# Delta rule: q's rows and the output's columns turned by VectorE blocks and GpSimd transfers through DRAM

## The chip, the cores and the metric

The kernel runs on one core of one Trainium2 chip. The core has TensorE (PE, matrix products into PSUM), VectorE (DVE), ScalarE (ACT), GpSimd (POOL) and SyncE (SP), and 16 DMA engines that the queues of SP, ACT and POOL share. The metric is the device time of one execution in microseconds (us): 2160.38 us as the median of 3 runs (2159.5 to 2160.82) for the kernel before.

## The reference

One inference step of a decoder layer for 512 prompt tokens and 8 sample tokens, width 2048. A normed input is multiplied with one matrix whose columns are q, k, v, an output gate z, two small gate columns, and the pooling channels. Eight heads of width 128 run a gated delta rule, four pooling groups run beside them; both go through one output matrix, and a SwiGLU block and a final norm follow. What the change touches, for each head of the prompt:

```python
q = l2norm(q) * (DN_HEAD_DIM ** -0.5)        # one factor for each token
...
# chunk by chunk:
v_new = u_i - einsum('bhck,bhkv->bhcv', w_i, S)
o = einsum('bhck,bhkv->bhcv', q_i * exp(g_i), S) + einsum('bhcs,bhsv->bhcv', qk_i, v_new)
S = S * exp(g_last) + einsum('bhck,bhcv->bhkv', k_dec, v_new)
...
dn_out = rmsnorm(o, dn_norm) * silu(z)
```

Products come out of the input projection with channels on partitions and tokens along the free dimension. The norm of q needs, for each token, the sum over channels, as a column with the token on the partition. The output o comes out with tokens on partitions, and the output projection needs it with channels on partitions.

## The kernel before

All matrix products are made in two float32r parts of each operand ("hi" and "lo"), three passes for each product. In the first part of the program, one "tile" is 128 output columns of the input matrix for all 520 tokens: 16 steps over the contraction, each with two column halves and three passes (lines 168 to 170), and the second half three steps behind the first. The weights come in granules of 128x1024 by SP's queue, are cut into hi by ScalarE (line 135) and lo by VectorE (line 137), and the products are evicted by VectorE (line 259).

After nearly each step `weave.step()` is called (class `Weave`): it runs generators on tracks, each of which issues a few small instructions and yields the number of steps until it goes on. So the small work of the heads stands between the matmuls of the big products, in the order in which the generators are run. For TensorE this order is kept as it is written; on the other engines a scheduler sets the order from what is issued, with priorities.

Two batches of four heads: for each batch four k tiles, four z tiles, and then for each head a q tile and a v tile, after which `delta(h, qT, vT)` is put on track 0. It takes some 26 steps, and so runs during the q and v tiles of the next head. It

- multiplies q with the decay (line 825), multiplies the inverse's parts (lines 831, 850) with the copy `xt_` between them (line 833, ScalarE) and `uu` (line 852, VectorE),
- turns q with four TensorE transposes (line 838), so that ScalarE sums the squares of each token out of PSUM (line 757, called at 840) and a root by GpSimd (line 215, called at 843) gives the factor `fq`,
- runs four chunks of 128 tokens, each with the matmuls of lines 877, 884, 889, 895 and 896, and the state `S` written by VectorE (line 892 for chunk 0, line 894 for others); line 877 of the next chunk waits for `S`,
- sums the squares of the output (line 902), takes the root `ro`, scales the output into `on`, a part of `mixb` (line 910), and puts `gate(h, on)` on track 1.

`gate` turns `on` with four TensorE transposes (line 916) and multiplies the result with the norm's weights and the gate (line 918) into `mix[h]`. After the heads come eight pooling tiles, with the last head's recurrence, the sample tokens' products and the pooling products (`pool_mix`, track 1) woven into them, and the output projection. The feed-forward part follows, and takes most of the time.

Of the kernel before, what the change touches and what calls it, by code (L numbers as in the profile page):

```python
# [8 lines left out]
F32 = mybir.dt.float32  # L9
F32R = mybir.dt.float32r  # L10
I32 = mybir.dt.int32
AF = mybir.ActivationFunctionType
# [21 lines left out]
HG = 8  # L34
BUFS = {
    "ext": 2, "y": 1, "ys": 1, "g3": 3, "junk": 1, "ss": 2, "rr": 2, "nb": 1, "u": 1, "tm": 2, "xt_": 1, "uu": 2,
    "qts": 1, "fq": 2, "aq": 1, "vs": 1, "R": 2, "W": 2, "S": 2, "so": 2, "ro": 2, "s0": 2, "s2": 1, "kd": 4, "st": 2,
}
SKEW = 3
AHEAD = 2000  # L40
# [2 lines left out]
class Weave:  # L43
# [1 line left out]


    def __init__(self):
        self.tracks, self.wait, self.now = ([], []), [0, 0], 0

    def add(self, task, track=0, delay=0):  # L50
        self.tracks[track].append((task, self.now + delay))
# [18 lines left out]
def decoder_kernel(ctx, tc, x_prompt, x_sample, state_delta, state_conv, state_pool, norm_mix, w_in,  # L70
# [17 lines left out]
    def pst():  # L88
        return ps_dn.tile([P, 512], F32, tag="dn", name="dn")
# [431 lines left out]
    with ExitStack() as p1:  # L521
# [204 lines left out]
        def ck(c):  # L726
            return slice(P * c, P * (c + 1))


        def qkv_tile(sec, h, out, ext=None):  # L730
# [9 lines left out]
            act.activation(out, y, AF.Silu)  # L740
            pool.tensor_copy(ccp[:, :, t], ext[:, SEQ:SEQ + 3])

        def decay(h):

            gcb = d1tile("g3", [P, SEQ], "gcb")
            sp.dma_start(gcb, gcr_d[h:h + 1, :].broadcast_to([P, SEQ]))
            dm = d1tile("g3", [P, SEQ], "dm")
            for c in range(NCH):
                dve.scalar_tensor_tensor(dm[:, ck(c)], gcb[:, ck(c)], gcs[:, c, h:h + 1], mneg,
                                         op0=ALU.subtract, op1=ALU.min)  # L750
            act.activation(dm, dm, AF.Exp)
            return gcb, dm
# [64 lines left out]
        def delta(h, qT, vT):  # L817
# [15 lines left out]
            act.copy(xt_, v3(xp)[:, :, 0:96])  # L833
            cur = d1tile("uu", [P, SEQ], "uu")
            pool.tensor_copy(v3(cur), udf)
            qtp = pst()
            for c in range(NCH):
                te.transpose(qtp[:, ck(c)], qT[:, ck(c)], ident)
            ss = d1tile("ss", [P, NCH], "ss")
            squares(qtp, ss)  # L840
            dve.tensor_scalar(ss, ss, EPS, None, op0=ALU.add)
            fq = d1tile("fq", [P, NCH], "fq")
            pow_mhalf(fq, ss)
            dve.tensor_scalar(fq, fq, float(P) ** -0.5, None, op0=ALU.mult)
            yield 2
            for it in range(3):
                yp = v3(pst())
# [24 lines left out]
            for c in range(NCH):  # L872
                if S is None:
                    R = vs[:, ck(c)]
                else:
                    kp = pst()
                    te.matmul(kp[:, 0:P], kT[:, ck(c)], S, start=True, stop=True)
                    Rt = d1tile("R", [P, P], "R")
                    dve.scalar_tensor_tensor(Rt, kp[:, 0:P], negc[:, c, h:h + 1], vs[:, ck(c)],
                                             op0=ALU.mult, op1=ALU.add)  # L880
                    R = Rt
                    yield 2
                wp = pst()
                te.matmul(wp[:, 0:P], cur[:, ck(c)], R, start=True, stop=True)
                W = d1tile("W", [P, P], "W")
                act.copy(W, wp[:, 0:P])
                yield 2
                dp = pst()
                te.matmul(dp[:, 0:P], kd[:, ck(c)], W, start=True, stop=True)
                S2 = d1tile("S", [P, P], "S")  # L890
                if S is None:
                    dve.tensor_copy(S2, dp[:, 0:P])
                else:
                    dve.scalar_tensor_tensor(S2, S, egl[:, c, h:h + 1], dp[:, 0:P], op0=ALU.mult, op1=ALU.add)
                    te.matmul(op_[:, ck(c)], qts[:, ck(c)], S, start=True, stop=False)
                te.matmul(op_[:, ck(c)], aq[:, ck(c)], W, start=(S is None), stop=True)
                S = S2
                yield 1
            sp.dma_start(nd_prompt[0, 0, h], S)

            so = d1tile("so", [P, NCH], "so")
# [6 lines left out]
            dve.tensor_tensor(ro, ro, fq, op=ALU.mult)  # L908
            on = nn
            dve.tensor_tensor(v3(on), v3(op_), bc3(ro), op=ALU.mult)  # L910
            weave.add(gate(h, on), 1, 8)

        def gate(h, on):
            otp = pst()
            for c in range(NCH):
                te.transpose(otp[:, ck(c)], on[:, ck(c)], ident)
            yield 1
            dve.scalar_tensor_tensor(mix[h][:, NB:NTOK], otp, dnw, mix[h][:, NB:NTOK], op0=ALU.mult, op1=ALU.mult)

# [167 lines left out]
        def qv_tiles(h):  # L1089
            utf = utfs[h % 2].rearrange("p a c j -> p (a c) j")  # L1090
            for q in range(4):
                r = slice(32 * q, 32 * q + 32)
                sp.dma_start(utf[r, :, r], ud_d[h, q].rearrange("a c s j -> s (a c) j"))
            qT = d1tile("s0", [P, SEQ], "qT")
            qkv_tile(0, h, qT)
            vT = d1tile("s2", [P, SEQ], "vT")
            qkv_tile(2, h, vT)
            weave.add(delta(h, qT, vT), 0, 1)

        kds = {}  # L1100
        for b in range(2):
            for h in range(4 * b, 4 * b + 4):
                qkv_tile(1, h, mixb[:, h % 4, 0:SEQ],
# [27 lines left out]
        for t in (6, 7, 4, 5, 2, 3, 0, 1):  # L1131
            pool_tile(t, operands)
            if t % 2:
                weave.add(pool_mix(t // 2, *splits[t // 2]), 1, 12 if t > 1 else 7)
        weave.add(pool_out(), 0, 6)

        order = [*range(8), 14, 15, 12, 13, 10, 11, 8, 9]
# [939 lines left out]
```

## Time and profile before

| what | value |
|---|---|
| median of 3 runs | 2160.38 us (2159.5 to 2160.82) |
| profiled execution, first to last instruction | 2158.9 us |
| TensorE busy | 2136.1 us (99%) |
| VectorE busy | 1746.4 us (81%) |
| ScalarE busy | 929.6 us (43%) |
| GpSimd busy | 433.8 us (20%) |
| the four recurrences of a batch (about) | 160 to 290 us, and 388 to 518 us |

Times in a timeline are us from the span's start; a row is start, duration, engine, line and instruction, and in brackets the idle time of the engine before it and what ended it. A matmul's duration runs from its start to the end of its flow through the array, so matmuls that follow each other overlap; the distance from one start to the next is what one takes from the engine. A group's row has busy time and mean ns of one, then the idle time before.

### The profile page before, as it was taken

The page shows a single profiled execution, that of the slowest core. Times are in us where ns is not written, and L with a number is a line of the kernel's source. Part 1 is how long each engine was busy: PE and PEld are TensorE (multiplying, and loading weights), DVE is VectorE, ACT ScalarE, POOL GpSimd, SP SyncE. Part 2 cuts the span into 40 slices and gives each one's busy share as a digit, 9 for nine tenths or more (in the row PEclk, how much of TensorE's full clock was granted, in tenths as well). Part 3 has the DMA queues.
Part 4 walks back from the last instruction along what each step waited for, and adds up shares of the span by engine and source line. Part 5 has one row for each costly group of instructions (what it writes and reads, how often), then busy time and mean ns, then how long its engine had stood idle before and what let it go on. Part 6 is the DMA issues. An engine that isn't in the chain of part 4 may idle for free.

```text
span 2158.9 us, 42980 instructions
## 1 busy us (share of the span) xinstructions
PE 2136.1 (99%) x17809; PEld 2128.8 (99%) x17809; DVE 1746.4 (81%) x2619; ACT 929.6 (43%) x1404; POOL 433.8 (20%) x512
## 2 busy tenths in 40 slices
PE   8999999999999999999999999999999999999998
PEld 7999999999999999999999999999999999999998
DVE  7786667666499979988988888888877898887997
ACT  6533443432264545434433434434334444435444
POOL 2210110111012202233233233232113302003100
PEclk9999999999999999999999999999999999999999
DMA  8343234323445543554554454454446746438343
GB/s 281 92 110 91 76 94 112 88 76 96 120 121 161 152 119 111 155 166 141 145 166 139 147 167 143 142 163 134 125 147 189 234 111 205 115 103 247 93 108 119
DMA packets 442497, 297.04 MB, mean 138 GB/s; under 512 B 26556, under 2 KB 423253, under 8 KB 438957
## 3 DMA queue, kind: packets, MB, share of 16 engines
q1 hardware_dynamic: 422733, 219.94, 36.3%
q0 software_dynamic: 18256, 73.55, 10.5%
q8 instruction: 139, 2.28, 0.5%
q10 hardware_dynamic: 1312, 0.80, 0.1%
q14 instruction: 57, 0.47, 0.1%
HBM read 251.47 MB, written 43.43 MB: 137 GB/s over the span
## 4 chain that ended last, share of the span: by engine, by line
PE 86%; DVE 8%; DMA 2%; issue 2%; ACT 1%; POOL 1%; SPq 0%; DVEq 0%; POOLq 0%; ACTq 0%
PE dn L1223 20%; PE dn L1222 20%; PE dn L1224 20%; PE mm L168 6%; PE mm L170 6%; PE mm L169 6%; DVE lo L1216 2%; DVE raw L1244 1%; PE dn L850 1%; DMA st<-a_d 1%; DVE lo L137 1%; POOL st L1776 0%; DMA xt<-in_x_prompt_dram 0%; PE dn L960 0%; PE dn L857 0%
## 5 line engine op out<-in xcount | busy, mean ns | idle before, releaser
L1215 ACT CAST hi<-raw 128x1024 fp32r<-128x1024 f32 (+1 forms) x422 | 427.4, 1027 | 400.2 <-DVE raw L1244 206.5
L1216 DVE TENSOR_TENSOR lo<-raw,hi 128x1024 fp32r<-128x1024 f32 (+1 forms) x422 | 527.4, 1270 | 87.1 <-ACT hi L1215 85.6
L168 PE MATMUL mm<-xh,hi 128*128 128x256 f32 (+1 forms) x1280 | 379.7, 297 | 2.4 <-DVE mixa L259 2.4
L169 PE MATMUL mm<-xl,hi 128*128 128x256 f32 (+1 forms) x1280 | 361.5, 282 | 0.9 <-DVE xl L350 0.7
L170 PE MATMUL mm<-xh,lo 128*128 128x256 f32 (+1 forms) x1280 | 361.8, 283 | 0.4 <-DVE lo L137 0.4
L168 PEld LDWEIGHTS mm<-xh,hi 128*128 128x128 f32 x1280 | 241.4, 189 | 3.7 <-DVE mixa L259 3.1
L169 PEld LDWEIGHTS mm<-xl,hi 128*128 128x128 f32 x1280 | 241.7, 189 | 1.7 <-DVE xl L350 1.7
L170 PEld LDWEIGHTS mm<-xh,lo 128*128 128x128 f32 x1280 | 240.8, 188 | 0.6 <-DVE lo L137 0.6
L1244 DVE TENSOR_TENSOR raw<-raw 128x1024 f32<-128x1024 f32 (+1 forms) x130 | 175.3, 1349 | 2.2
L1223 PE MATMUL dn<-b21l,hi 128*128 128x260 f32 x620 | 175.7, 283 | 0.4 <-DVE b21l L1786 0.4
L1224 PE MATMUL dn<-b21h,lo 128*128 128x260 f32 x620 | 175.4, 283 | 0.0
L1222 PE MATMUL dn<-b21h,hi 128*128 128x260 f32 x620 | 175.0, 282 | 0.0
L1224 PE MATMUL dn<-b11h,lo 128*128 128x260 f32 x612 | 173.4, 283 | 1.2 <-DVE lo L1216 1.1
L1223 PE MATMUL dn<-b11l,hi 128*128 128x260 f32 x612 | 173.3, 283 | 0.0
L1222 PE MATMUL dn<-b11h,hi 128*128 128x260 f32 x612 | 172.7, 282 | 0.0
L1222 PE MATMUL dn<-T1h,hi 128*128 128x260 f32 x556 | 158.1, 284 | 0.0
L1223 PE MATMUL dn<-T1l,hi 128*128 128x260 f32 x556 | 157.7, 284 | 0.0
L1224 PE MATMUL dn<-T1h,lo 128*128 128x260 f32 x556 | 156.7, 282 | 0.0
L1222 PE MATMUL dn<-B22h,hi 128*128 128x260 f32 x548 | 155.9, 284 | 0.0
L1223 PE MATMUL dn<-B22l,hi 128*128 128x260 f32 x548 | 155.6, 284 | 0.0
L1224 PE MATMUL dn<-B22h,lo 128*128 128x260 f32 x548 | 154.6, 282 | 0.4 <-DVE lo L1216 0.4
L135 ACT CAST hi<-raw 128x1024 fp32r<-128x1024 f32 (+2 forms) x86 | 87.1, 1014 | 148.2 <-PE mm L169 139.4
(659 smaller groups left out, 6422.5 us busy)
## 6 DMA issues: line engine op xcount, KB each, us to landing
raw<-in_w_gate_up_dram SPq DMA_DIRECT2D x134, 512.0 KB
raw<-in_w_in_dram SPq DMA_DIRECT2D x79, 512.0 KB
a_d<-mixa POOLq DMA_DIRECT2D x22, 1040.0 KB, 5.5
raw<-in_w_down_dram SPq DMA_DIRECT2D x48, 448.0 KB
mixb<-in_w_gate_up_dram SPq DMA_DIRECT2D x41, 512.0 KB
raw<-in_w_out_dram SPq DMA_DIRECT2D x25, 512.0 KB
st<-a_d POOLq DMA_DIRECT2D x49, 260.0 KB, 6.5
raw<-in_w_down_dram SPq DMA_DIRECT2D x24, 512.0 KB
```

The source lines that it names most:

```text
L135: act.copy(hi[:, r], raw[:, r])
L137: dve.tensor_tensor(lo[:, r], raw[:, r], hi[:, r].bitcast(F32), op=ALU.subtract)
L168: te.matmul(acc[ci], wh, hi[k][:, c0:c1], start=(k == 0), stop=False)
L169: te.matmul(acc[ci], wh, lo[k][:, c0:c1], start=False, stop=False)
L170: te.matmul(acc[ci], wl, hi[k][:, c0:c1], start=False, stop=(k == len(w) - 1))
L850: te.matmul(yp[0:96, c, j], xt_[:, c, :], udf[:, c, j] if it == 0 else v3(cur)[:, c, j], start=True, stop=True)
L1215: act.copy(hi, raw)
L1216: dve.tensor_tensor(lo, raw, hi.bitcast(F32), op=ALU.subtract)
L1222: te.matmul(acc, wh[:, k, :], xf[:, k, :], start=start and k == 0, stop=False)
L1223: te.matmul(acc, wh[:, k, :], xg[:, k, :], start=False, stop=False)
L1224: te.matmul(acc, wl[:, k, :], xf[:, k, :], start=False, stop=stop and k == wh.shape[1] - 1)
L1244: dve.tensor_tensor(r[name], r[a], r[b], op=op)
```

## The change

For each head, q's turned rows and the output's turned columns are now made without TensorE. A transpose on VectorE turns each block of 32x32 inside a 128x512 tile; a store by GpSimd's queue puts that into DRAM; four loads by the same queue, one for each 32 partitions, put the blocks into their places.

- `query_rows` (lines 751 to 759, track 2) starts 5 steps after the q tile: block transpose (753), store in rows of 2 KB (754), and 6 steps later four loads in runs of 512 bytes (759) into a new tile `qk`. The squares of q (923) are taken of this tile, and the root `fq` is issued behind chunk 0 of the recurrence.
- `output_columns` (lines 761 to 770, track 2) starts 6 steps after the recurrence: block transpose of `on` (764), store in runs of 512 bytes (765), and 6 steps later four loads in runs of 128 bytes (769) back into `on`. `gate` then goes on track 3 with a delay of 8 steps, and its product (944) reads `on` from SBUF.
- The transposes of k and v stay on TensorE. `Weave` has four tracks for two, the first `pool_mix` is delayed by 20 steps for 12, and the room for the descriptors of GpSimd's queue is set to 8192 bytes.

```diff
-        self.tracks, self.wait, self.now = ([], []), [0, 0], 0
+        self.tracks, self.wait, self.now = ([], [], [], []), [0] * 4, 0
...
+        tok_d = dram.tile([2, H, P, SEQ], F32, name="tok_d")
...
+        def query_rows(h, qT):
+            bt, d = d1tile("bt", [P, SEQ], "bt"), tok_d[0, h]
+            dve.transpose(bt.rearrange("p (j c q) -> p c j q", j=4, c=NCH), qT.rearrange("p (c j q) -> p c j q", j=4, c=NCH))
+            pool.dma_start(d, bt)
+            yield 6
+            rows = d.rearrange("(i p) (j f) -> j p i f", p=32, j=4)
+            qk = qks[h] = d1tile("tq", [P, SEQ], "qk")
+            for j in range(4):
+                pool.dma_start(qk[32 * j:32 * j + 32, :].rearrange("p (n q) -> p n q", n=4), rows[j])
+
+        def output_columns(h, on):
+            bt = d1tile("bt", [P, SEQ], "bt")
+            d = tok_d[1, h].rearrange("p f -> (p f)").rearrange("(c p f) -> c p f", c=NCH, p=P)
+            dve.transpose(bt, on)
+            pool.dma_start(d.rearrange("c p f -> p c f"), v3(bt))
+            yield 6
+            rows = d.rearrange("c (i p) (j q) -> j p (c i) q", p=32, q=32)
+            for j in range(4):
+                pool.dma_start(on[32 * j:32 * j + 32, :].rearrange("p (n q) -> p n q", q=32), rows[j])
+            weave.add(gate(h, on), 3, 8)
...
-            qtp = pst()
-            for c in range(NCH):
-                te.transpose(qtp[:, ck(c)], qT[:, ck(c)], ident)
-            ss = d1tile("ss", [P, NCH], "ss")
-            squares(qtp, ss)
...
+                if c == 0:
+                    ss = d1tile("ss", [P, NCH], "ss")
+                    junk = d1tile("junk", [P, P], "junk")
+                    for j in range(NCH):
+                        act.activation(by_column(junk), by_chunk(qks[h])[:, j], AF.Square, accum_out=ss[:, j:j + 1])
...
-            weave.add(gate(h, on), 1, 8)
+            weave.add(output_columns(h, on), 2, 6)
 
         def gate(h, on):
-            otp = pst()
-            for c in range(NCH):
-                te.transpose(otp[:, ck(c)], on[:, ck(c)], ident)
             yield 1
-            dve.scalar_tensor_tensor(mix[h][:, NB:NTOK], otp, dnw, mix[h][:, NB:NTOK], op0=ALU.mult, op1=ALU.mult)
+            dve.scalar_tensor_tensor(mix[h][:, NB:NTOK], on, dnw, mix[h][:, NB:NTOK], op0=ALU.mult, op1=ALU.mult)
...
+            weave.add(query_rows(h, qT), 2, 5)
...
-                weave.add(pool_mix(t // 2, *splits[t // 2]), 1, 12 if t > 1 else 7)
+                weave.add(pool_mix(t // 2, *splits[t // 2]), 1, 20 if t == 7 else 12 if t > 1 else 7)
...
-    nc = _bacc.Bacc("TRN2", target_bir_lowering=False, num_devices=1)
+    nc = _bacc.Bacc("TRN2", target_bir_lowering=False, num_devices=1, dynamic_dma_scratch_size=8192)
```

How the instructions stand on the engines that wait, before and now, at three places. First VectorE, from the multiplication of the inverse in head 2's recurrence to the first state of that recurrence (`uu` is the inverse, `vs` the scaled v, `mixa` head 1's gated output, `S` the state). Before:

```order
L852 SCALAR_TENSOR_TENSOR uu<-dn,utf_645 96x4x96
L860 SCALAR_TENSOR_TENSOR aq<-dn,sck,dm 128x128 x4
L918 SCALAR_TENSOR_TENSOR mixa<-dn,prm,mixa 128x512
L852 SCALAR_TENSOR_TENSOR uu<-dn,utf_645 96x4x64
L867 TENSOR_TENSOR vs<-dn,sck 128x512
L852 SCALAR_TENSOR_TENSOR uu<-dn,utf_645 96x4x32
L137 TENSOR_TENSOR lo<-raw,hi 128x1024
L892 COPY S<-dn 128x128
L879 SCALAR_TENSOR_TENSOR R<-dn,negc,vs 128x128
```

and now, at the same place (after a block transpose of head 1's output, line 764, some rows earlier):

```order
L872 SCALAR_TENSOR_TENSOR uu<-dn,utf_645 96x4x96
L880 SCALAR_TENSOR_TENSOR aq<-dn,sck,dm 128x128 x4
L872 SCALAR_TENSOR_TENSOR uu<-dn,utf_645 96x4x64
L887 TENSOR_TENSOR vs<-dn,sck 128x512
L872 SCALAR_TENSOR_TENSOR uu<-dn,utf_645 96x4x32
L927 TENSOR_SCALAR fq<-fq 128x4
L933 TENSOR_TENSOR ro<-fq 128x4
L137 TENSOR_TENSOR lo<-raw,hi 128x1024
L944 SCALAR_TENSOR_TENSOR mixa<-mixb,prm,mixa 128x512
L912 COPY S<-dn 128x128
L899 SCALAR_TENSOR_TENSOR R<-dn,negc,vs 128x128
```

The gated product went from the middle of the inverse to the place right before the copy of the state. Second, GpSimd around the same time, between the root `ro` of head 1's output and the clear of the `ext` tile after the next. Before:

```order
L835 COPY uu<-utf_647 128x512
L215 TENSOR_TENSOR ro<-so,mhalf 128x4
L741 COPY ccp<-ext 128x3
L263 MEMSET ext 128x3
L215 TENSOR_TENSOR fq<-ss,mhalf 128x4
L741 COPY ccp<-ext 128x3
```

and now:

```order
L754 DMA tok_d<-bt 128x512
L759 DMA qk<-tok_d 32x4x128 x4
L864 COPY uu<-utf_647 128x512
L215 TENSOR_TENSOR ro<-so,mhalf 128x4
L741 COPY ccp<-ext 128x3
L765 DMA tok_d<-bt 128x4x128
L769 DMA mixb<-tok_d 32x16x32 x4
L215 TENSOR_TENSOR fq<-ss,mhalf 128x4
L263 MEMSET ext 128x3
L741 COPY ccp<-ext 128x3
```

Each group of loads stands right behind its store, which it waits for, and the root `fq`, the clear and the next copy stand behind the loads. Third, ScalarE at the beginning of head 2's recurrence (`gcb` is the decay's exponential, `qk` q's rows). It had the copy of `xt_` ahead of the squares; now:

```order
L135 CAST hi<-raw 128x1024
L923 ACTIVATE junk,ss<-qk 128x128
L852 ACTIVATE gcb<-gcb 128x512
L923 ACTIVATE junk,ss<-qk 128x128
L862 COPY xt__2932<-dn 128x384
L923 ACTIVATE junk,ss<-qk 128x128 x2
L740 ACT_TABLE_LOAD
```

Two of the four squares, which wait for q's loads, now stand ahead of that copy.

More of the change, by code (lines that the diff above doesn't have):

```diff
@@ L36 @@
     "ext": 2, "y": 1, "ys": 1, "g3": 3, "junk": 1, "ss": 2, "rr": 2, "nb": 1, "u": 1, "tm": 2, "xt_": 1, "uu": 2,
-    "qts": 1, "fq": 2, "aq": 1, "vs": 1, "R": 2, "W": 2, "S": 2, "so": 2, "ro": 2, "s0": 2, "s2": 1, "kd": 4, "st": 2,
+    "qts": 1, "fq": 2, "aq": 1, "vs": 1, "bt": 2, "tq": 1, "R": 2, "W": 2, "S": 2, "so": 2, "ro": 2, "s0": 2, "s2": 1, "kd": 4, "st": 2,
 }
@@ L741, in qkv_tile, with by_chunk, by_column @@
             pool.tensor_copy(ccp[:, :, t], ext[:, SEQ:SEQ + 3])
+        tok_d = dram.tile([2, H, P, SEQ], F32, name="tok_d")
+        def by_chunk(a):
+            return a.rearrange("p (i c q) -> p c i q", i=4, c=NCH)
+        def by_column(a):
+            return a.rearrange("p (i q) -> p i q", i=4)
+        def query_rows(h, qT):
[17 more added lines that the diff above has]
+            weave.add(gate(h, on), 3, 8)
         def decay(h):
@@ L835, in delta @@
             pool.tensor_copy(v3(cur), udf)
-            qtp = pst()
-            for c in range(NCH):
-                te.transpose(qtp[:, ck(c)], qT[:, ck(c)], ident)
-            ss = d1tile("ss", [P, NCH], "ss")
-            squares(qtp, ss)
[L841 to L844, printed above, removed]
             yield 2
@@ L898, in delta @@
                 yield 1
+                if c == 0:
[3 more added lines that the diff above has]
+                        act.activation(by_column(junk), by_chunk(qks[h])[:, j], AF.Square, accum_out=ss[:, j:j + 1])
+                    dve.tensor_scalar(ss, ss, EPS, None, op0=ALU.add)
+                    fq = d1tile("fq", [P, NCH], "fq")
+                    pow_mhalf(fq, ss)
+                    dve.tensor_scalar(fq, fq, float(P) ** -0.5, None, op0=ALU.mult)
             sp.dma_start(nd_prompt[0, 0, h], S)
@@ L1098, in qv_tiles @@
             weave.add(delta(h, qT, vT), 0, 1)
-        kds = {}
+        kds, qks = {}, {}
         for b in range(2):
```

## The prediction

> **What bounds the kernel now.** I read the page's busy times and slices, then a table of windows, the chain, and timelines of the delta stage, where the change sits. First the page's line 1 and the TensorE row of the 40 slices (the delta stage is slices 4 to 10), and two rows of the window table for the two runs of heads (columns: us, then busy us of PE, PEld, DVE, ACT, POOL, clock, DMA share, GB/s), with a third for the end of the out-projection:
>
> ```profile
> PE 2136.1 (99%) x17809; PEld 2128.8 (99%) x17809; DVE 1746.4 (81%) x2619; ACT 929.6 (43%) x1404; POOL 433.8 (20%) x512
> PE   8999999999999999999999999999999999999998
> 150.00:284.00 134.00, 134.00 (x1166) 134.00 (x1165) 84.95 (x188) 56.68 (x120) 13.43 (x31) 1.00 0.33 87
> 380.00:530.00 150.00, 150.00 (x1301) 149.91 (x1300) 95.57 (x219) 55.87 (x130) 15.80 (x32) 1.00 0.31 82
> 640.00:700.00 60.00, 58.85 (x489) 58.44 (x488) 57.32 (x69) 30.00 (x37) 16.56 (x18) 1.00 0.54 161
> ```
>
> In both runs of heads TensorE has no idle microsecond at a full clock, while VectorE is busy 84.95 of 134 us (63%), ScalarE 42%, GpSimd 10%, and the DMA engines 0.33. So this stage ends when TensorE has issued its instructions. What leaves TensorE there shortens the kernel, as long as nothing that TensorE waits for comes later than its slack. After the pool tiles the program's order on every engine is what it was, so the rest of the kernel only starts earlier.
>
> **What is removed.** Two transpose groups of four per head, lines 838 (q) and 916 (output). Each line's own view gives the count, TensorE's timeline what a group holds, and the last row is one piece of the chain (start, us):
>
> ```profile
> L838 PE MATMUL dn<-ident,qT x32: 272/272/273, 162.8 to 485.1; 128*128 128x128 f32 x32
> L916 PE MATMUL dn<-ident,mixb x32: 270/272/273, 198.0 to 518.3; 128*128 128x128 f32 x32
> 226.65 0.60 PE L838 MATMUL dn<-ident,qT 128*128 128x128 f32 x4
> 227.00 0.36 PE L168 MATMUL mm<-xh,hi 128*128 128x264 f32 x1
> 227.21 0.28 PE L169 MATMUL mm<-xl,hi 128*128 128x264 f32 x1
> 227.33 0.28 PE L170 MATMUL mm<-xh,lo 128*128 128x264 f32 x1
> 230.13 0.60 PE L916 MATMUL dn<-ident,mixb 128*128 128x128 f32 x4
> 230.48 0.37 PE L168 MATMUL mm<-xh,hi 128*128 128x264 f32 x1
> ...
> 517.82 0.28 PE L170 MATMUL mm<-xh,lo 128*128 128x256 f32 x1
> 517.95 0.60 PE L916 MATMUL dn<-ident,mixb 128*128 128x128 f32 x4
> ...
> 226.81 0.44 PE dn L838 x4
> ```
>
> Matmuls overlap, so the 272 ns of one is no price. From the group's first start to the next matmul's start are 227.00 - 226.65 = 0.35 us and 230.48 - 230.13 = 0.35 us. 64 instructions are 16 groups: 16 x 0.35 = 5.6 us, and with the starts in full (0.355 us) 5.7 us. The 0.21 us between the next two starts, against 0.12 us from L169 to L170, follows every group of another kind; it falls away only where L916 stands alone between ordinary matmuls, as at 517.95 for head 7, and so at head 3 (2 x 0.09 us). **I take 5.9 us.** The bound above is what a group adds to the chain, 0.44 us, which makes 7.0 us; below, 5.6.
>
> The Trainium skill ("TensorE: Matmul & The Clock Gate", Part 4: PE-mode transpose) gives a transpose in a kernel's context about 275 ns. By that, 64 would give back 17.6 us; the trace has the same duration in its rows (272 ns) but starts four in 0.35 us, and I go by the starts.
>
> **What is added, and where it lies.**
>
> *VectorE* gets two block transposes (lines 753 and 764) of 128x512 per head. No such operation is in the trace; the nearest rows are these, with the line-918 product that now reads the output from SBUF as line 944:
>
> ```profile
> L737 DVE TENSOR_SCALAR y<-ext,prm 128x512 f32<-128x512 f32 x20 | 10.6, 528 | 0.4
> L910 DVE TENSOR_TENSOR mixb<-dn,ro 128x512 f32<-128x512 f32 x8 | 5.5, 690 | 0.2
> L918 DVE SCALAR_TENSOR_TENSOR mixa<-dn,prm,mixa 128x512 f32<-128x512 f32 x8 | 5.9, 739 | 0.0
> L739 DVE SCALAR_TENSOR_TENSOR y<-ext,prm,y 128x512 f32<-128x512 f32 x60 | 44.9, 748 | 1.0
> L137 DVE TENSOR_TENSOR lo<-raw,hi 128x1024 fp32r<-128x1024 f32 x51 | 62.3, 1222 | 40.6 <-ACT hi L135 40.4
> ```
>
> Between 0.53 us (one input, same size) and 1.22 us (twice the size); I take 0.69. Line 944 is 0.75 from SBUF (L739) for 0.74. That is 1.4 us more per head of 32 us, 63% to 68% busy: hidden. ScalarE's four squares per head only change their source. The 24 matmuls of the first pool product come eight steps later, with four pool tiles still to follow: nothing.
>
> *GpSimd* gets ten DMAs per head. Issue and landing, from groups on GpSimd and DMA issues (the last number of an issue is us to landing, the median):
>
> ```profile
> L1429 POOL DMA_DIRECT2D out_dram<-ub x16 | 12.8, 803 | 4.7 <-POOL ub L1428 4.7
> L1500 POOL DMA_DIRECT2D h_d<-mixa x8 | 4.5, 557 | 54.5 <-DVE mixa L1488 54.5
> L1411 POOL DMA_DIRECT2D a_d<-mixa x22 | 12.6, 571 | 6.5 <-POOL mixa L1410 6.5
> out_dram<-ub POOLq DMA_DIRECT2D x16, 256.0 KB, 3.1
> h_d<-mixa POOLq DMA_DIRECT2D x8, 260.0 KB, 3.6
> nt<-in_state_conv_dram POOLq DMA_DIRECT2D x1, 256.0 KB, 5.5
> q1 hardware_dynamic: 422733, 219.94, 36.3%
> ```
>
> A transfer in rows of 128 runs costs 0.56 us to issue, one in 512 runs 0.80. Query: one store and four reads of 128 runs, 5 x 0.56; output: 5 x 0.80; together 6.8 us of GpSimd per 32 us, where it is busy 3.2 now. The DMA engines get 3,200 runs per head; at the 29.7 ns that a packet of the first queue holds an engine (36.3% of 16 x 2158.9 us over 422,733) that is 5.9 us per engine, so the share goes from 0.33 to about 0.52, less than the 0.54 of the third window, where TensorE is still 98% busy. [...] All of it is hidden, if the landings are in time. That is the open point, because each read waits for its store on GpSimd's queue, and the results are waited for by instructions with urgent work behind them.
>
> *Place 1: VectorE before chunk 0's state* (head 1's output, while head 2's recurrence starts):
>
> ```profile
> 224.43 0.69 DVE L910 TENSOR_TENSOR mixb<-dn,ro 128x512 f32<-128x512 f32 x1
> 225.04 0.41 DVE L259 TENSOR_TENSOR ext<-mm,rb 128x256 f32<-128x256 f32 x1
> 232.38 0.74 DVE L918 SCALAR_TENSOR_TENSOR mixa<-dn,prm,mixa 128x512 f32<-128x512 f32 x1
> 235.37 0.29 DVE L852 SCALAR_TENSOR_TENSOR uu<-dn,utf 96x128 f32<-96x128 f32 x1 [1.33 <-PE dn L850]
> 237.13 1.23 DVE L137 TENSOR_TENSOR lo<-raw,hi 128x1024 fp32r<-128x1024 f32 x1 [1.48 <-ACT hi L135]
> 238.77 0.29 DVE L892 COPY S<-dn 128x128 f32<-128x128 f32 x1 [0.41 <-PE dn L889]
> 239.51 0.38 PE L877 MATMUL dn<-S,mixb 128*128 128x128 f32 x2
> ```
>
> In this clock: block transpose 225.45 to 226.14; its store is issued then and lands 3.1 us later, 229.24; four reads of 0.80 us follow, the last issued at 231.64 and landed 3.1 us later, 234.7. The product (line 944) now stands between L137 and the copy of S; VectorE gets to it at 237.13 + 1.23 = 238.36, so it has 3.6 us to spare. It ends at 239.11, S starts 0.34 us later than now and ends at 239.40, and L877 wants it at 239.51: about a tenth to spare. I charge 0.05 us for each of the six heads with this order (0, 1, 2, 4, 5, 6): **0.3 us**. If a landing takes 5.5 us, the reads are there at 226.14 + 5.5 + 2.4 + 5.5 = 239.54, S ends at 240.58, and TensorE stands 1.1 us. Behind the store on GpSimd's queue wait only the fq root, two clears of ext and the next ccp copy; the root's reader (line 927) comes at 235.66, two us after the last read is issued.
>
> *Place 2: ScalarE before the xt_ copy* (head 2's q). The squares (line 923) now wait for q's reads, ahead of the copy that TensorE's L850 needs:
>
> ```profile
> 214.40 0.63 ACT L740 ACTIVATE qT<-y 128x512 f32<-128x512 f32 x1
> 215.80 0.35 DVE L894 SCALAR_TENSOR_TENSOR S<-S,egl,dn 128x128 f32<-128x128 f32 x1 [1.43 <-PE dn L889]
> 224.35 1.04 ACT L135 CAST hi<-raw 128x1024 fp32r<-128x1024 f32 x1
> 226.85 0.48 ACT L833 COPY xt__2915<-dn 128x384 f32<-128x384 f32 x1 [0.93 <-PE dn L831]
> 228.53 0.84 PE L850 MATMUL dn<-utf,xt__2915 128*96 128x96 f32 x8
> ```
>
> qT ends at 215.03, its block transpose at 215.72, just ahead of the S update at 215.80 (the 1.43 us of idle time take it). Store landed 218.8, last read issued 220.5, landed 223.6; the squares are reached at 225.39. 1.8 us to spare, and the copy has another 1.2 us before L850. At 5.5 us a landing the reads come at 228.4 and L850 stands about 1.5 us.
>
> **The sum.** 2158.9 - 5.9 + 0.3 = 2153.3 us of span. The median of the runs, 2160.38, lies 1.5 us over the profiled span; so I forecast 2160.38 - 5.6 = **2154.8 us**, 0.26% less.
>
> **Rivals.**
>
> *B, half eaten.* Landings about 5 us: store 231.14, last read 233.54, landed 238.54, the product 0.2 us late; at place 2 the reads come at 227.4 and L850 stands about 0.7 us. One late wait shifts the other, so some 0.5 us over seven heads: 2154.8 + 3.5 = 2158.3 us. For it the 5.5 us row; against it, the rows of 3.1 and 3.6 us.
>
> *C, slower: the reads land after VectorE gets to the product.* At 6 us a landing the product starts at 240.54, S ends at 241.58 and L877 stands 2.1 us; six heads are 12.6 us: 2154.8 + 12.6 = 2167.4 us. It turns into a loss where a head loses over 0.9 us, at landings of some 5.4 us. Nothing in the stage shows a read of 128-byte runs from GpSimd. The Trainium skill ("DMA: Bandwidth & Descriptors", Specifications) puts the line rate at 512 bytes and more, with a read-modify-write below; the output's reads move 128-byte runs, and no run so far shows whether GpSimd's suffer.
>
> *D, nothing changes.* TensorE's time is given back by a chain outside it (casts of weights, evictions): 2160.4 us. Against it: not one wait of TensorE in either run of heads.
>
> *E, more is won.* A transpose holds TensorE for its whole 272 ns: 64 x 0.272 = 17.4 us, 2143 us. Against it, the starts above. The 275 ns of the Trainium skill would mean this.
>
> **How the numbers follow.** Forecast 0.62, B 0.20, C 0.10, D 0.06, E 0.02. A measurement here can tell about 0.2% (4.3 us) from no change: faster is below 2156.1, that is the forecast, E and the edge of B, 0.65; the same is the rest of B and D, 0.25; slower C, 0.10. The forecast's own range is 2153.7 (the 7.0 us bound, less the slips) to 2156.0. To leave out no more than two in ten the range goes on over B: 2153.6 to 2160.0.
>
> **What would show it.** Right: TensorE's busy time lower by about the 64 instructions and no new wait of it in the delta stage; block transposes of about 0.7 us; POOL landings of 3 to 4 us; line 944 not waiting for a DMA. Wrong: TensorE waiting at the S matmul (L897 of the new kernel) or at the product with xt_; VectorE idle before line 944, or ScalarE before line 923, released by a DMA.

## The result, and the profile after

The changed kernel takes 2156.9 us (median of 18 runs, 2156.01 to 2158.36), the kernel before 2160.88 us (18 runs, 2159.5 to 2162.13) beside it. The ratio is 0.9982, with a 95% interval of 0.9975 to 0.9989: 4.0 us less (2.4 to 5.4). The forecast was 2154.8 us. The profiled execution's span is 2154.4 us against 2158.9.

The page's first line, and the two runs of heads in the window table (columns as in the prediction):

```profile
PE 2129.6 (99%) x17745; PEld 2121.1 (98%) x17745; DVE 1759.6 (82%) x2635; ACT 929.0 (43%) x1404; POOL 481.9 (22%) x592
...
150.00:284.00 134.00, 133.34 (x1156) 133.13 (x1154) 91.78 (x196) 56.79 (x124) 36.67 (x66) 1.00 0.43 115
380.00:530.00 150.00, 149.45 (x1290) 149.07 (x1289) 103.36 (x232) 55.75 (x131) 39.87 (x73) 1.00 0.41 112
```

TensorE's 64 matmuls are gone. But where it had no idle microsecond before, it now lacks 0.66 and 0.55 us. GpSimd's load in the first window rose from 13.43 to 36.67 us, the DMA share from 0.33 to 0.43. TensorE's waits between 60 and 760 us (sum in us, times, longest) name what is new:

```profile
PE mm L168 <- DVE mixa L259: 2.6, 3, 1.3
...
PE dn L870 <- ACT xt__2146 L862: 0.7, 1, 0.7
PE dn L870 <- DVE uu L872: 0.5, 1, 0.5
```

The first stood there before (2.4 us). The two of L870 are new: the inverse's product (L870, before L850) waits once for the copy of xt_ (ScalarE) and once for uu (VectorE).

The added work itself, in groups (busy us, mean ns), and the transfers (the last number is median us from issue to landing):

```profile
L753 DVE STREAM_TRANSPOSE bt<-qT 128x512 f32<-128x512 f32 x8 | 5.7, 712 | 5.6 <-ACT qT L740 5.6
L764 DVE STREAM_TRANSPOSE bt<-mixb 128x512 f32<-128x512 f32 x8 | 5.6, 703 | 0.0
L759 POOL DMA_DIRECT2D qk<-tok_d x32 | 17.5, 555 | 15.7 <-DMA tok_d<-bt 15.0 <-issue 0.6
L769 POOL DMA_DIRECT2D mixb<-tok_d x32 | 20.9, 658 | 13.7 <-DMA tok_d<-bt 13.2 <-issue 0.5
L923 ACT ACTIVATE junk<-qk 128x128 f32<-128x128 f32 x32 | 9.8, 307 | 6.9 <-DMA qk<-tok_d 6.5
L944 DVE SCALAR_TENSOR_TENSOR mixa<-mixb,prm,mixa 128x512 f32<-128x512 f32 x8 | 6.0, 747 | 0.0
...
tok_d<-bt POOLq DMA_DIRECT2D x16, 256.0 KB, 2.8
qk<-tok_d POOLq DMA_DIRECT2D x32, 64.0 KB, 2.7
mixb<-tok_d POOLq DMA_DIRECT2D x32, 64.0 KB, 3.1
```

The gated product (L944) never waits for its reads. The squares (L923) do: ScalarE stood 6.5 us in three stretches (heads 0, 4 and 7) until q's reads had landed.

**A ruler finer than the runs.** All kernels here issue the same 3,840 main matmuls of the input projection and the pooling tiles (L168 to L170) in the same order, so the n-th start of one trace can be set against the n-th of another. Differences below are of that kind. "Stage" is the time from the 961st such matmul (at 160.09 us before) to the 3,292nd (518.30 us before), which holds all eight recurrences; "tail" is from there to the 3,840th. Ahead of the stage (the 961st starts at 159.7 to 161.5 us in these traces) and behind the tail (1543.1 to 1545.3 us to the last matmul) single profiled executions differ by up to 2 us with no order in it, so spans are not compared.

| kernel | stage, us | tail, us | median, us | ratio (95%) |
|---|---|---|---|---|
| before | 358.21 | 89.59 | 2160.9 | |
| changed | 353.33 | 89.94 | 2156.9 | 0.9982 (0.9975 to 0.9989) |
| changed, again | 353.67 | 89.81 | 2157.3 | 0.9984 (0.9975 to 0.9994) |
| nothing turned | 352.36 | 90.02 | 2155.8 | 0.9977 (0.9968 to 0.9986) |
| squares behind xt_ | 353.59 | 90.19 | 2155.6 | 0.9978 (0.9969 to 0.9986) |
| q only | 358.15 | 89.76 | 2160.9 | 1.0000 (0.9990 to 1.0009) |
| output only | 355.08 | 90.02 | 2157.8 | 0.9986 (0.9977 to 0.9996) |
| squares behind chunk 1 | 351.42 | 90.06 | 2154.7 | 0.9970 (0.9959 to 0.9981) |
| q only, squares behind chunk 1 | 354.80 | 89.69 | 2157.4 | 0.9984 (0.9975 to 0.9993) |
| first heads' q on TensorE | 353.04 | 89.97 | 2156.0 | 0.9977 (0.9968 to 0.9986) |
| reads issued 12 steps on | 354.18 | 89.86 | 2157.4 | 0.9985 (0.9976 to 0.9994) |
| groups issued twice | 365.39 | 89.72 | 2168.4 | 1.0037 (1.0022 to 1.0052) |
| side parts alone | 358.19 | 89.82 | 2160.8 | 1.0002 (0.9992 to 1.0011) |
| output's reads made thrice | 356.12 | 94.86 | 2162.8 | 1.0012 (1.0002 to 1.0022) |

The n-th starts, before against changed, give this account. At each of the sixteen places where a group was removed the changed kernel gains 0.40 to 0.45 us, 6.8 us together. It loses 0.90 us at head 0's inverse, 0.33 at head 4's and 0.56 at head 7's, and 0.1 to 0.2 us in steps too small to place: 4.88 us of stage are left. The tail gives back 0.35. Stage and tail together are 4.5 us shorter, inside the runs' interval of 2.4 to 5.4 us.

### The profile page after: what moved, and what is told of

It reads as the page before. It is cut to its first block, busy times and chain, and to the rows that moved or that the text cites. A ratio compares the mean times of both kernels' runs of the same rounds, so it can differ in the third digit from the quotient of the medians.

```text
span 2154.4 us, 43035 instructions
## 1 busy us (share of the span) xinstructions
PE 2129.6 (99%) x17745; PEld 2121.1 (98%) x17745; DVE 1759.6 (82%) x2635; ACT 929.0 (43%) x1404; POOL 481.9 (22%) x592
## 3 DMA queue, kind: packets, MB, share of 16 engines
q0 software_dynamic: 21584, 81.95, 12.0%
## 4 chain that ended last, share of the span: by engine, by line
PE 85%; DVE 8%; DMA 2%; ACT 2%; issue 2%; POOL 1%; DVEq 0%; ACTq 0%; POOLq 0%; SPq 0%
PE dn L1250 21%; PE dn L1249 21%; PE dn L1251 21%; PE mm L168 6%; PE mm L170 5%; PE mm L169 5%; DVE lo L1243 1%; DVE lo L137 1%; PE dn L870 1%; DMA st<-a_d 1%; DVE raw L1271 1%; POOL st L1803 0%; DVE tm L836 0%; PE dn L986 0%; DVE u L838 0%
## 5 line engine op out<-in xcount | busy, mean ns | idle before, releaser
L168 PE MATMUL mm<-xh,hi 128*128 128x256 f32 (+1 forms) x1280 | 379.5, 297 | 2.6 <-DVE mixa L259 2.6
L169 PE MATMUL mm<-xl,hi 128*128 128x256 f32 (+1 forms) x1280 | 361.6, 283 | 0.9 <-DVE xl L350 0.5
L170 PE MATMUL mm<-xh,lo 128*128 128x256 f32 (+1 forms) x1280 | 361.7, 283 | 0.4 <-DVE lo L137 0.4
L168 PEld LDWEIGHTS mm<-xh,hi 128*128 128x128 f32 x1280 | 241.4, 189 | 3.8 <-DVE mixa L259 3.2
L169 PEld LDWEIGHTS mm<-xl,hi 128*128 128x128 f32 x1280 | 241.7, 189 | 1.7 <-DVE xl L350 1.7
L170 PEld LDWEIGHTS mm<-xh,lo 128*128 128x128 f32 x1280 | 240.9, 188 | 0.6 <-DVE lo L137 0.6
L1435 POOL TENSOR_TENSOR mixa<-mixa 128x520 f32<-128x520 f32 x22 | 51.3, 2330 | 495.5 <-DVE mixa L1429 495.5
```

The source lines that it names most:

```text
L168: te.matmul(acc[ci], wh, hi[k][:, c0:c1], start=(k == 0), stop=False)
L169: te.matmul(acc[ci], wh, lo[k][:, c0:c1], start=False, stop=False)
L170: te.matmul(acc[ci], wl, hi[k][:, c0:c1], start=False, stop=(k == len(w) - 1))
L1435: pool.tensor_tensor(q[:, 4:8:2, :], q[:, 1:4:2, :], q[:, 0:2, :], op=ALU.subtract)
```

## Why heads 0 and 4

ScalarE and TensorE of the changed kernel, head 0 and head 2 at the same work:

```profile
154.20 0.63 ACT L740 ACTIVATE qT<-y 128x512 f32<-128x512 f32 x1 [4.43 <-DVE y L739]
...
161.90 1.03 PE L860 MATMUL dn<-utf,mixb 128*128 128x96 f32 x8
...
163.80 0.31 ACT L923 ACTIVATE junk<-qk 128x128 f32<-128x128 f32 x1 [2.53 <-DMA qk<-tok_d]
...
164.54 0.46 ACT L862 COPY xt__2146<-dn 128x384 f32<-128x384 f32 x1
165.06 0.92 PE L870 MATMUL dn<-utf,xt__2146 128*96 128x96 f32 x8 [0.67 <-ACT xt__2146 L862]
...
214.06 0.63 ACT L740 ACTIVATE qT<-y 128x512 f32<-128x512 f32 x1
...
224.97 0.30 ACT L923 ACTIVATE junk<-qk 128x128 f32<-128x128 f32 x1
225.43 1.03 PE L860 MATMUL dn<-utf,mixb 128*128 128x96 f32 x8
```

In head 2, q is ready at 214.69 and TensorE begins the inverse (L860) 10.7 us later; in head 0, q is ready at 154.83 and the inverse begins 7.1 us later. The first head of a batch has no recurrence of an earlier head woven into its v tile, so TensorE gets there 3.7 us sooner, and block transpose, store and reads (about 9 us) no longer fit between. Head 4 has 7.6 us and shows the same: its copy of xt_ ends at 387.97 us behind two squares, and L870 starts at 388.02. So two squares that wait for reads stand ahead of the copy of xt_ on ScalarE, and TensorE waits behind both.

## The experiments

**1. Nothing turned.** The squares and the gated product take q and the output as they lie; no block transposes, no transfers. The kernel leaves out both turnings by that: it sums the squares of q over tokens, and the gate takes the output with tokens on partitions.

```diff
-                        act.activation(by_column(junk), by_chunk(qks[h])[:, j], AF.Square, ...)
+                        act.activation(by_column(junk), by_column(qT[:, ck(j)]), AF.Square, ...)
...
-            weave.add(output_columns(h, on), 2, 6)
+            weave.add(gate(h, on), 3, 20)
...
-            weave.add(query_rows(h, qT), 2, 5)
```

> The changed kernel without block transposes and without the ten transfers per head: the squares read q as it lies (channels on partitions), the gated product reads the output as it lies, 20 steps after the recurrence as before. So the sixteen TensorE groups are gone and nothing takes their place (the norm of q and the gated output are wrong, the work is otherwise the same). Theory 1 (a group is worth 0.40 to 0.45 us of TensorE, 6.8 us for sixteen, and the new kernel gives back 1.8 us at three late waits, heads 0, 4 and 7): all 6.8 us stay, span near 2152.1 us, median near 2154 us. Theory 2 (a group is worth the 0.355 us from its first start to the next, 5.9 us in all, as the prediction took): span 2153.0 us. Theory 3 (a transpose holds TensorE for 272 ns): span 2141 us.

Measured: each group 0.41 to 0.45 us again, theory 1's price (0.35 at head 0's q); no loss at heads 0 and 4. But 0.78 us are still lost at head 7, so the stage is 352.36 us, 5.85 us gained of 6.8. Theory 1 had called head 7's wait a cost of the transfers; here it stands without any. Its rows on VectorE and TensorE:

```profile
481.65 0.17 DVE L927 TENSOR_SCALAR fq<-fq 128x4 f32<-128x4 f32 x1 [0.50 <-POOL fq L215]
...
482.66 0.25 DVE L933 TENSOR_TENSOR ro<-fq 128x4 f32<-128x4 f32 x1
...
484.40 0.55 DVE L872 SCALAR_TENSOR_TENSOR uu<-dn,utf 96x384 f32<-96x384 f32 x1
...
485.09 0.86 PE L870 MATMUL dn<-uu,xt__6032 128*96 128x64 f32 x8 [0.68 <-DVE uu L872]
```

VectorE reaches uu behind the root of q's squares, for which it idles 0.50 us, and TensorE, two groups ahead of its old time, is there first.

**2. The halves apart.** In "q only" the output keeps its TensorE group, in "output only" q does.

```diff
 # q only
-            weave.add(output_columns(h, on), 2, 6)
+            weave.add(gate(h, on), 1, 8)          # with te.transpose of `on`, as before
...
 # output only
-            weave.add(query_rows(h, qT), 2, 5)    # and qtp, squares(qtp, ss), fq as before
```

> Only q goes through VectorE blocks and DRAM; the output is turned on TensorE as before. Theory 1: eight groups at 0.41 us are gained (3.3 us) and 1.2 us given back at heads 0 and 4 (0.90 and 0.33): span near 2156.8 us, ratio about 0.9990. Theory 2 (0.355 us a group and slips of 0.05 us a head at the first state): 2.8 us gained and nothing returned, span 2156.1 us.

> Only the output goes through VectorE blocks and DRAM; q is turned on TensorE as before. Theory 1: eight groups at 0.44 us are gained (3.5 us) and at most head 7's 0.56 us given back: span 2155.4 to 2156.0 us, ratio about 0.9985. Theory 2 (0.355 us a group and 0.3 us of slips at the first state, which belong to this half): 2.8 + 0.2 - 0.3, span 2156.2 us. A late landing (rival C of the prediction) would show as VectorE idle before line 944 of this kernel's gated product.

Measured: the output's half gains 3.13 us of stage (eight steps of 0.42 to 0.45, with 0.3 given back), and its gated product waits for nothing, as theory 1 has it. The q half gains 0.06: neither theory foresaw that. Each of its groups gains 0.41 us, and at the inverse of six heads 0.25 to 0.99 us are lost, 3.2 together. In heads 0, 4 and 6 it is the copy of xt_ again (0.8 and 0.5 us of waiting in heads 0 and 6; in head 4 the copy ends at 390.83 us and L870 starts at 390.88); in heads 1, 2 and 5 it is uu. VectorE in the kernel before, then VectorE and TensorE in "q only", head 1:

```profile
197.14 0.16 DVE L841 TENSOR_SCALAR ss<-ss 128x4 f32<-128x4 f32 x1
198.44 0.17 DVE L844 TENSOR_SCALAR fq<-fq 128x4 f32<-128x4 f32 x1 [1.14 <-POOL fq L215]
...
198.76 0.55 DVE L852 SCALAR_TENSOR_TENSOR uu<-dn,utf 96x384 f32<-96x384 f32 x1
```

```profile
198.32 0.16 DVE L924 TENSOR_SCALAR ss<-ss 128x4 f32<-128x4 f32 x1
199.63 0.17 DVE L927 TENSOR_SCALAR fq<-fq 128x4 f32<-128x4 f32 x1 [1.14 <-POOL fq L215]
...
199.95 0.55 DVE L872 SCALAR_TENSOR_TENSOR uu<-dn,utf 96x384 f32<-96x384 f32 x1
...
200.65 0.86 PE L870 MATMUL dn<-uu,xt__2535 128*96 128x64 f32 x8 [0.21 <-DVE uu L872]
```

Sum and root of q stand ahead of uu in both, with 1.14 us of idle VectorE. Before, uu ended at 199.31 and TensorE took it at 199.86, 0.55 us to spare. Here sum and uu are 1.2 us later, TensorE's inverse only 0.41 (its first product, L870, starts at 196.78 for 196.37), so uu is 0.78 us later against it; 0.55 were spare, and TensorE idles 0.21 us. In the changed kernel heads 1, 2, 3, 5 and 6 have the root behind uu. The halves don't add up, because each leaves the engines in another order.

**3. Squares held back behind xt_.** The squares write their unused products into xt_, and so wait for TensorE's last read of it.

```diff
-                    junk = d1tile("junk", [P, P], "junk")
+                    junk = xt_.rearrange("p c j -> p (c j)")[:, 0:P]
```

> The changed kernel, only that the squares of q write their unused products into xt_, so that ScalarE can't take them before TensorE has read xt_ for the last time; every transfer stays. Theory 1 (1.8 us are given back because squares that wait for q's reads stand ahead of the copy to xt_, and because the sums and roots behind them stand ahead of uu on VectorE in head 7): waits of L870 on xt_ and uu go from 1.2 us to under 0.2 us, span 2152.4 to 2153.0 us, median some 1.5 to 1.8 us under the changed kernel's 2156.9. Rival (the transfers themselves take the time, by what they do to the weight stream): nothing moves, span 2154.4 us, median 2156.9 us.

Measured: the waits for xt_ and uu are gone, but the stage is 353.59 us, no better than the changed kernel. The theory named the waits rightly and not what came next: the root now stands ahead of chunk 0's S. VectorE, then TensorE, head 0:

```profile
176.20 0.17 DVE L927 TENSOR_SCALAR fq<-fq 128x4 f32<-128x4 f32 x1 [1.16 <-POOL fq L215]
...
176.49 0.28 DVE L912 COPY S<-dn 128x128 f32<-128x128 f32 x1
...
176.83 0.49 PE L897 MATMUL dn<-S,mixb 128*128 128x128 f32 x2 [0.55 <-DVE S L912]
```

0.81 us are lost there in head 0, 0.80 in head 4, 0.46 in head 3. (The median is 2155.6 us; the interval holds the changed kernel's.)

**4. Squares behind chunk 1,** where the next S is some 4 us off; on the changed kernel, and with the output on TensorE.

```diff
-                if c == 0:
+                if c == 1:
                     ss = d1tile("ss", [P, NCH], "ss")
-                    junk = d1tile("junk", [P, P], "junk")
+                    junk = aq[:, ck(0)]
```

> The changed kernel, only that the squares of q are issued behind chunk 1 and write their unused products into the part of aq that chunk 0 has read last, so ScalarE takes them between the W copies of chunks 0 and 1, and VectorE their sums and root ahead of chunk 1's S, not ahead of uu or of chunk 0's S. Theory 1 (what the delta stage gives back are order waits of these squares and their roots): no wait of TensorE on xt_, uu or S in heads 0 to 6, the stage (first matmul step of head 0's v tile end to the end of head 7's inverse, 358.2 us before and 353.3 us in the changed kernel) 351.8 to 352.4 us, median 2154.5 to 2155.5 us. Rival (the give-back moves to another wait, as it did when the squares stood ahead of chunk 0's S: 353.6 us): stage 353 us or more.

> Only q goes through VectorE blocks and DRAM, with the squares and the root behind chunk 1 as in the run beside it; the output is turned on TensorE. Theory 1 (the q half alone gained nothing, 358.15 against 358.21 us of stage, because the sum and the root of q stood ahead of uu on VectorE and cost 0.4 us a head, not because of its transfers): now eight groups at 0.41 us are gained, stage 354.9 us, ratio about 0.9985. Rival (the five transfers per head cost what eight groups bring): stage 358 us, ratio 1.000.

Measured: 351.42 us of stage, 6.79 less than before and 0.4 below theory 1's range, and 354.80 with q alone, 3.41 less than before. With both halves, TensorE's waits between 60 and 760 us, all of them, and the two windows:

```profile
PE mm L168 <- DVE mixa L259: 3.0, 3, 1.7
PE dn L1251 <- DVE lo L1243: 1.2, 2, 1.0
PE dn L169 <- DVE dl L195: 0.4, 1, 0.4
PE dn L986 <- DMA s<-in_state_delta_dram: 0.3, 1, 0.3
...
150.00:284.00 134.00, 134.00 (x1163) 134.00 (x1163) 92.01 (x196) 58.66 (x127) 36.35 (x66) 1.00 0.44 116
380.00:530.00 150.00, 150.00 (x1299) 150.00 (x1298) 102.84 (x230) 56.70 (x130) 40.58 (x73) 1.00 0.42 112
```

Not one wait is left in the heads, with every transfer in place: TensorE is busy 134.00 of 134 and 150.00 of 150 us, and all sixteen groups are won. So neither the transfers nor the block transposes cost anything in the stage; the order behind the squares did. The median is 2154.7 us. The ratio's interval and the changed kernel's overlap, so the runs alone do not tell these two apart; the stage does, with 351.42 us in its one trace and 353.33 and 353.67 in the changed kernel's two.

**5. The first heads' q on TensorE,** the others through DRAM.

```diff
-            weave.add(query_rows(h, qT), 2, 5)
+            if h % 4:
+                weave.add(query_rows(h, qT), 2, 5)     # h 0 and 4: qtp, squares(qtp, ss), fq as before
```

> The changed kernel, only that in heads 0 and 4 q is turned on TensorE as before; the other six heads take the way through DRAM. Theory 1 (in the first head of a batch the v tile holds no recurrence, so TensorE reaches the inverse some 4 us sooner after q's tile, before q's reads have landed; that cost 0.90 and 0.33 us): both waits go and two groups come back, 0.82 us: stage 353.3 - 1.23 + 0.82 = 352.9 us. Rival (the late reads are those of every head, and heads 0 and 4 only show it first): the wait moves to heads 1 and 5, stage 353.5 us or more.

Measured: 353.04 us. Both late steps are gone and don't move to heads 1 and 5; head 7's is 0.73. That the first head of a batch is special holds.

**6. A group's price.** The kernel before, each group issued twice in a row.

```diff
-            for c in range(NCH):
+            for c in (*range(NCH), *range(NCH)):
                 te.transpose(qtp[:, ck(c)], qT[:, ck(c)], ident)     # and so for otp
```

> The kernel before, only that each of the sixteen groups is issued twice in a row, into the same place. Theory 1 (a group is worth 0.42 us because it takes the 0.355 us between starts and makes the next matmul's start 0.07 to 0.09 us later, which a group beside another group doesn't do again): the second set adds 16 x 0.34 to 0.36 us, stage 358.2 + 5.4 to 5.8 = 363.6 to 364.0 us. If the whole 0.42 us came again: 364.9 us. Rival E of the prediction (272 ns of TensorE for each transpose): stage 375.6 us, median some 2178 us.

Measured: steps of 0.43 to 0.45 us at each of the sixteen places, stage 365.39 us, 7.2 more (0.35 of it between the batches). Theory 1's 0.34 to 0.36 for a second set was wrong, and so was its reason. TensorE at head 1's output, and the same place before in the prediction:

```profile
231.41 1.04 PE L916 MATMUL dn<-ident,mixb 128*128 128x128 f32 x8
232.20 0.37 PE L168 MATMUL mm<-xh,hi 128*128 128x264 f32 x1
232.40 0.28 PE L169 MATMUL mm<-xl,hi 128*128 128x264 f32 x1
```

Eight transposes hold the next matmul off for 0.79 us, four did for 0.35: four more are 0.44, 109 ns each. In the trace the starts inside a group follow each other at 109 ns, the matmul behind it is recorded only 28 ns after the last of them, and its own successor 0.20 us later (the last two rows) where ordinary ones follow at 0.12. So first start to next start is short of the steady distance by some 0.08 us whatever the group's length, and four more transposes take 4 x 109 ns. Rival E's 272 ns is out.

**7. The side parts alone:** the kernel before with the room for descriptors and the later pooling product.

```diff
-                weave.add(pool_mix(t // 2, *splits[t // 2]), 1, 12 if t > 1 else 7)
+                weave.add(pool_mix(t // 2, *splits[t // 2]), 1, 20 if t == 7 else 12 if t > 1 else 7)
...
-    nc = _bacc.Bacc("TRN2", target_bir_lowering=False, num_devices=1)
+    nc = _bacc.Bacc("TRN2", target_bir_lowering=False, num_devices=1, dynamic_dma_scratch_size=8192)
```

> The kernel before, only with the room for GpSimd's descriptors at 8192 bytes and the first pooling product 20 steps behind its tile instead of 12. Theory 1 (both cost nothing): stage 358.2 us, from there to the last pooling tile 89.6 us within 0.1, ratio 1.000. Rival (the later pooling product is where the 0.35 us of that stretch went, 89.94 us in the changed kernel): 89.9 us or more there.

Measured: stage 358.19, tail 89.82 us: 0.23 us more, between the two. It arises at a wait for a sample state: TensorE idles 0.2 us in this trace (L960 for `s`), 0.1 in the changed kernel, and 0.3 to 0.6 in four of the others. In the changed kernel that load is issued by SP at 540.10 us right behind two weight loads, lands at 544.7, and TensorE takes it at 544.77; before it landed 1.2 us ahead of its use. The tails of the kernels with the later pooling product lie between 89.69 and 90.19 us (experiment 9 aside), and those of the two without it are 89.59 and 89.72; what shifts them from one to the other is not settled.

**8. Reads 12 steps behind the store,** the product's place kept.

```diff
             pool.dma_start(d.rearrange("c p f -> p c f"), v3(bt))
-            yield 6
+            yield 12
...
-            weave.add(gate(h, on), 3, 8)
+            weave.add(gate(h, on), 3, 2)
```

> The changed kernel, only that the four reads of the output are issued 12 steps behind the store instead of 6, and the gated product 2 steps behind them instead of 8, so its place stays. This makes the reads land some 5 us later. Rival C of the prediction (a read that lands after VectorE gets to the gated product holds chunk 0's S and TensorE behind it): in head 1 the reads landed 1.9 us ahead of the product in the changed kernel, so now 3 us behind; S and TensorE lose 2 to 3 us in each of six heads, stage 365 to 371 us, median 2169 to 2175 us. Against it (VectorE has room, others cover it): stage 353 us, as the changed kernel.

Measured: no test of rival C. GpSimd issued head 1's last read at 232.64 us for 231.55, only 1.1 us later: in these traces a read goes once its store has landed and GpSimd is free (head 1's store in the changed kernel landed at 229.32 us, its first read started at 229.61), and a later place in the code moved it behind one root, no more. The stage is 354.18 us; TensorE waits 1.2 us for uu, against 0.5 in the changed kernel, with the roots in other places.

**9. Reads made three times,** on the kernel of experiment 4.

```diff
-            for j in range(4):
-                pool.dma_start(on[32 * j:32 * j + 32, :]..., rows[j])
+            for t, j in [(t, j) for t in (x1, x2, on) for j in range(4)]:       # x1, x2: spare tiles
+                pool.dma_start(t[32 * j:32 * j + 32, :]..., rows[j])
```

> The kernel with the squares behind chunk 1, only that the four reads of the output are made three times, twice into spare tiles and then into their place: eight more transfers of 64 KB per head, 5.2 us more of GpSimd, and the gated product ready some 5 us later; VectorE has it behind chunk 2 instead of ahead of chunk 0's S. Theory 1 (the transfers lie beside other work; only an instruction that waits for them ahead of urgent work costs): stage 351.4 to 352.0 us. Rival (the transfers cost by what they take from the weight stream and from GpSimd): 3,072 more runs of 128 bytes and more for each head show in the stage, 353 us or more.

(Eight transfers of 64 KB are 4,096 runs of 128 bytes, not 3,072.) Measured: both, at different places; the stage is 356.12 us. In the runs of heads nothing: from the 961st to the 1,756th main matmul 129.82 us in both kernels, and 128.30 in both from the 2,501st to the 3,292nd, with 5.2 us more of GpSimd per head. Between the batches 4.7 us are lost, and 4.8 in the tail. The row of the second elimination's start, in the kernel of experiment 4 and here, and TensorE's waits here:

```profile
337.66 0.20 DVE L836 TENSOR_TENSOR tm<-nb,u 64x31 f32<-64x31 f32 x1 [1.26 <-DMA nb<-nd_d]
```

```profile
344.82 0.20 DVE L836 TENSOR_TENSOR tm<-nb,u 64x31 f32<-64x31 f32 x1 [4.88 <-DMA nb<-nd_d]
...
PE mm L168 <- DVE mixa L259: 5.5, 4, 3.0
PE dn L986 <- DMA s<-in_state_delta_dram: 3.2, 3, 2.5
```

The load of the elimination's input (nb) is issued by SP at 337.3 us for 333.9, VectorE idles for it with the eviction of a z tile (L259) behind it, and TensorE waits 3.0 us for that. The load also lands later: 7.5 us after its issue, for 3.8. Here SP issues a weight load 0.6 us ahead of it, there one 1.1 us behind it; whether that is what slows it was not tested. In the tail 3.2 us of TensorE's waits are for the sample states. On GpSimd head 3's spare reads stand between the next batch's clears (L820) and roots of k (L215), which lead to that load; the steps between were not followed one by one. So room on GpSimd is free in the heads and not between the batches. Rival C's own case, a late read held in front of chunk 0's S, was not made by this either: VectorE has the gated product behind chunk 2 here.

**10. The changed kernel once more.**

> The changed kernel itself, for a second trace. Theory 1 (its three waits are set by the order, not by chance): late steps of 0.9 us at head 0, 0.2 to 0.4 at head 4, 0.5 to 0.6 at head 7, stage 353.1 to 353.6 us. Rival (chance landings): other heads or sizes, stage off by more than 0.5 us.

Measured: 1.17 us at head 0, 0.92 at head 7, 0.10 at head 4; stage 353.67, just outside what theory 1 said. The same three heads come back, as the order would have it; the sizes differ by 0.2 to 0.4 us between the two traces, more than theory 1 allowed.

## Why the prediction was right, and where not

The time lies in the range (2153.6 to 2160.0) and 0.9 us above the forecast's own range; the direction is right, the size 4.0 us for 5.6. The interval of the ratio excludes 1, but at 0.18% the change is just under the 0.2% from which the prediction counted it as faster: the case given 0.25. That the forecast lies so near is in part luck, because two errors work against each other: 0.9 us too little for the groups, and some 1.8 us of losses that it put at 0.3 and at another place.

- **What bounds the kernel.** Right: with the waits taken away, all of what left TensorE left the stage (experiment 4).
- **What is removed: 5.9 us.** Mis-sized. Sixteen groups measured 6.8 us, some 0.41 us each for q and 0.44 for the output, near the upper bound of 7.0 from the chain's 0.44 us. The step that failed is the price "from the group's first start to the next matmul's start". The argument on the 0.21 us behind a group was right: they stay where another group stands in front. But the start ahead of these 0.21 us is early, and that too moves to the group in front. TensorE at head 0's q, in the kernel before and in the changed one:

```profile
161.90 1.03 PE L831 MATMUL dn<-utf,mixb 128*128 128x96 f32 x8
162.76 0.60 PE L838 MATMUL dn<-ident,qT 128*128 128x128 f32 x4
163.12 0.37 PE L168 MATMUL mm<-xh,hi 128*128 128x264 f32 x1
163.32 0.28 PE L169 MATMUL mm<-xl,hi 128*128 128x264 f32 x1
```

```profile
161.90 1.03 PE L860 MATMUL dn<-utf,mixb 128*128 128x96 f32 x8
162.71 0.37 PE L168 MATMUL mm<-xh,hi 128*128 128x264 f32 x1
162.92 0.28 PE L169 MATMUL mm<-xl,hi 128*128 128x264 f32 x1
```

The main matmul (L168) comes 0.41 us sooner, not 0.36, because it follows the group in front after 0.81 us where the first transpose followed after 0.86; L169 comes some 0.2 us behind it in both.
- **VectorE.** Right: 0.71 and 0.70 us for 0.69, L944 0.747 for 0.75.
- **GpSimd and DMA.** Near: 48 us in all, 6.0 per head, for 6.8; a share of 0.43 and 0.41 for 0.52. Landings of 2.7 to 3.1 us for 3.1. The count of 3,200 runs per head did not become as many packets: GpSimd's queue has 21,584 packets for 18,256, 416 more per head, so the price of 29.7 ns for each run does not carry over. "Hidden" holds in the heads; experiment 9 shows where it would not have.
- **Place 1: 0.3 us.** Nothing. In head 1's output the last read landed at 235.19, L944 began at 237.07, S ended at 238.01 and TensorE wanted it at 238.30. (By the prediction's own times the reader of the root comes 4.0 us after the last read is issued, 235.66 against 231.64, not two; nothing rests on it.)
- **Place 2: nothing charged.** This step failed. It was worked out on head 2 with 1.8 us to spare; there 0.4 us were (last read landed 224.53, squares reached at 224.97), and heads 0 and 4, with 3.7 and 3.2 us less between q and the inverse, were not looked at: 0.90 and 0.33 us. ScalarE idle ahead of line 923, released by a DMA, was among the prediction's own signs of being wrong: it idled 6.5 us.
- **The root of q.** The prediction moved it with the squares at no cost. In head 7 it stands ahead of uu, which cost 0.56 us with TensorE two groups early; without any transfer 0.78 us were lost there (experiment 1), and with the squares behind chunk 1 nothing (experiment 4).
- **The pooling product: nothing.** The tail is 0.35 and 0.22 us longer in the changed kernel's two traces and 0.23 with the side parts alone, but also 0.13 in experiment 6, which has none of them; what it costs is not settled.
- **Rivals.** B is the nearest to what happened: of the 1.79 us lost in the stage 1.23 came by its mechanism (a late read at place 2), at heads 0 and 4 alone; its landings of 5 us were not needed. C did not occur: the reads in runs of 128 bytes landed in 3.1 us, those of 512 bytes in 2.7 (medians). The Trainium skill ("DMA: Bandwidth & Descriptors", Specifications) warns of a read-modify-write below 512 bytes. The two kinds of reads here differ by 0.4 us in the median; no run separates what part of that it has. D and E are out.

## What to carry to other kernels

Price what is taken off a pipelined engine by the steady distance of starts inside the group times its count (here 4 x 109 ns, or 7.0 us for sixteen groups, where 6.8 were won), and test it by issuing the group twice. When work is moved to a way with long latency, check the slack at the iteration where the consumer comes soonest, such as the first of a batch, and not only in the steady state. The big instructions were hidden; what cost time were small ones that waited for them (a sum, a root of four columns) in front of urgent work on the same engine, and giving them a later dependency won back 1.9 us of stage.

## What was not expected

Each half's gain depends on the other: 0.06 and 3.13 us alone, 4.88 together, 3.41 for the q half alone with its root moved. A place later in the code did not make GpSimd issue a read later by more than 1.1 us. And the first start behind a group of transposes comes some 0.08 us early in the trace, which hides a fifth of what a group costs.
